# A decoder step on one core: split order, one PSUM pool, two plain gate columns, low parts on DVE, 17 groups by seven

## The chip, the cores and the metric

One core of one Trainium2 chip runs the whole program. The metric is device time in microseconds (us) of one launch; the median of three runs before the change is 1559.41 us (1559.0 to 1563.05). The core has five engines with a queue each, worked in order: TensorE (PE, matmul, with PEld for its weight loads), VectorE (DVE), ScalarE (ACT), GpSimd (POOL, which here also issues most small DMAs) and SyncE (SP, which issues the weight loads).

## The reference

A layer for 512 prompt tokens and 8 sample tokens (T = 520 columns): h = rmsnorm(x); one projection h @ w_in gives q, k, v, indexer queries, weights and key, the gate paths z_a and z_b, u, v of a gMLP, and the merge gates g_a, g_b (2048 columns each).

```python
o_a = prompt_attention(...)            # top-k by the indexer, softmax; sample_attention gathers from a paged cache
o_b = gmlp_mix(u, vb, ...)
y_a = (o_a * silu(z_a)) @ w_proj_a
y_b = (o_b * silu(z_b)) @ w_proj_b
mix = sigmoid(g_a) * y_a + sigmoid(g_b) * y_b
y   = rmsnorm(x + mix @ w_out)
```

All is float32. A product of two float32 matrices is made of three matmuls: each operand is split into a high part (float32r, rounded) and a low part (the rest), and high x high, high x low and low x high are summed in PSUM.

## The kernel before, in words

The activations stand transposed, features on partitions, as `hT_hi` and `hT_lo` (16 tiles of 128 features by 520 tokens). Weights stream in as `raw` tiles of 1 MB (1024 rows, 256 columns; three buffers, `load_raw`, on SP's queue). The work of TensorE is a flat list of chunks, built by `group` and `sgroup` and numbered in the order in which they run. A plain chunk has 8 k-tiles x 3 passes x 2 token halves = 48 matmuls of 260 columns; a plain group of 256 output columns over 2048 features has 4 chunks (192 matmuls). A group "by seven" (`by_seven`, `SEVEN`) makes the same output by Strassen's scheme (in Winograd's form): 7 chunks of 24 matmuls (168), whose weights are sums of the four quarter blocks b11, b12, b21, b22 of two raw tiles, made in place on DVE (`raw<-raw`), and whose moving operands are sums of the quarters of h. Those, forms 3, 5 and 7 (`Fh`, `Fl`) and form 6 (written over a quarter of hT), are made once by `build_forms`, some DVE sums and a split for each.

The program is one loop over chunks; iteration i issues, in this order, on every engine's queue: the split of a chunk ahead (ACT rounds `raw` to `whi`, DVE takes `wlo` = raw - whi: `hilo`; three chunks ahead in the stage by seven, `SLOOK`, two elsewhere, `LOOK`; four buffers `wspl`, so the split of chunk i+3 needs chunk i-1 done on TensorE), the evacuation of the chunk before (`pending`), chunk i's matmuls, and then one step of each running generator in `jobs` (attention, sample attention, loads, forms), in the order of their start. In the stage by seven the evacuation (`seven_after`) stands ahead of the split. So what an engine does is fixed at build time; a wait in one step holds whatever stands behind it on the same engine. Small tiles come from one pool `t` of 37 slots of 520 columns; a new tile waits until a slot is free.

PSUM: `pss` has four banks for attention and the like. The other four are `mains`: a pool of two pairs of banks (`pm`, plain chunks: both token halves, one bank each) or of four single banks (`pone`, chunks by seven). `banks` closes one pool and opens the other when the kind changes, which happens at the first chunk by seven and at the first one of the projection behind them.

Order of the chunks around the change: 92 to 107 q (8 heads); 108 to 111 z_a columns 0 and 1 (`plain_za(0)`, `evac_za`: Silu, then `gate_a` multiplies with the attention output `oT`, loaded back from DRAM by POOL, and stores to `oda`); 112 to 127 the first projection y_b = o_b @ w_proj_b (its operand `ob` is loaded and split by `loads_for_yb`, which starts with the evacuation of head 6; its results go to DRAM by `evac_yb`); 128 to 131 z_a columns 2 and 3; 132 to 257 the 18 groups by seven (z_a 4 to 7, g_b 0 to 15, g_a 0 to 15, two columns a group); 258 on the second projection y_a (operand `oa`, `loads_for_ya`), then w_out. For g_b each finished column is multiplied with y_b, loaded back from DRAM (`times_branch`). Beside chunks 108 to 123 `sample_attend` runs: for each of 8 samples POOL gathers the chosen keys and values from the cache (two indirect DMAs of about 1 us each for keys, two for values), DVE transposes the keys (`kTs`), ACT rounds them (`kTh`, line 1483), POOL subtracts (`kTl`, line 1484), TensorE multiplies (`ssP`, line 1474).

Lines that matter: 85 (all DVE work goes by `sub`, `add`, `mul`), 147 (the rounding of `hilo`), 337 (matmuls by seven), 352 (plain matmuls), 366 to 384 (`seven_after`), 1230 (`evac_yb`), 1394 (`evac_za`), 133 to 135 (`mm3`: attention).

Of the kernel before, what the change touches and what calls it, by code (L numbers as in the profile page):

```python
# [14 lines left out]
P = 128  # L15
# [25 lines left out]
WIKI_AT = 4  # L41
SEL_AT = 40
XR_AT = 10
COLS_N = NS + 2 * P
ROWS = (3, 0)
FIN = ("dve", "act", "pool", "pool")
# [13 lines left out]
def kernel(  # L60
# [31 lines left out]
    wspl = ctx.enter_context(tc.tile_pool(name="wspl", bufs=4))  # L92
    pools = {}
    dram = ctx.enter_context(tc.tile_pool(name="scratch", bufs=1, space=bass.MemoryType.DRAM))
    pss = ctx.enter_context(tc.tile_pool(name="pss", bufs=4, space=bass.MemoryType.PSUM))
    ctx.enter_context(tc.manual_schedule())
    mains = {}


    def banks(kind):  # L100
        if mains.get("kind") == kind:
            return
        if "cm" in mains:
            mains["cm"].__exit__(None, None, None)
        mains["n"] = mains.get("n", 0) + 1
        cm = tc.tile_pool(name=f"psm{mains['n']}", bufs=2 if kind == "pair" else 4, space=bass.MemoryType.PSUM)
        mains.update(kind=kind, cm=cm, pool=cm.__enter__())

    def pair_banks():
        banks("pair")  # L110
        return mains["pool"].tile([P, 2, 512], F32, name="pm")

    def one_bank():
        banks("one")
        return mains["pool"].tile([P, 512], F32, name="pone")

    xp = x_prompt[0]
    xs = x_sample.rearrange("b o d -> (b o) d")
# [132 lines left out]
    def split_steps(i, pieces):  # L251
        if i >= len(chunks) or not chunks[i]["new"]:
            return
        ch = chunks[i]
        hi = wspl.tile([P, 8, P], F32R, name="whi")
        lo = wspl.tile([P, 8, P], F32R, name="wlo")
        if ch.get("seven"):
            spl_tiles[ch["raw"], ch["step"]] = (hi, lo)
            a, b = raw_tiles[ch["raw"]], raw_tiles[ch["raw"] + 1]
            b11, b12, b21, b22 = a[:, :, :P], a[:, :, P:], b[:, :, :P], b[:, :, P:]  # L260
            step = ch["step"]
            hilo(hi, lo, (b11, b11, b12, b22, b21, b22, b21)[step])
            if step == 0:
                add(b11, b11, b12)
                add(b12, b12, b22)
            elif step == 3:
                add(b22, b11, b22)
                load_raw()
            elif step == 4:
                add(b21, b22, b21)  # L270
            elif step == 6:
                del raw_tiles[ch["raw"]], raw_tiles[ch["raw"] + 1]
                load_raw()
            return
        if ch["rows"]:
            hi, lo = (t.rearrange("p (k u) c -> p k (u c)", u=2) for t in (hi, lo))
            spl_tiles["rows", ch["kq"]] = (hi, lo)
            k0 = ch["kq"] % 2 * 4
            hilo(hi, lo, raw_tiles[ch["raw"]][:, k0:k0 + 4, :])
            if k0:  # L280
                del raw_tiles[ch["raw"]]
                load_raw()
            return
        src = raw_tiles[ch["raw"]][:, :, ch["c0"]:ch["c0"] + P]
        spl_tiles[ch["raw"], ch["u"]] = (hi, lo)
        n = 8 // pieces
        for k in range(0, 8, n):
            if ch["evac"] is packed:
                nc.scalar.activation(hi[:, k:k + n], src[:, k:k + n], AF.Copy)
                sub(hi[:, k:k + n, NIH:2 * NIH], src[:, k:k + n, :NIH], f32(hi[:, k:k + n, :NIH]))  # L290
            else:
                hilo(hi[:, k:k + n], lo[:, k:k + n], src[:, k:k + n])
            if k + n < 8:
                yield
        if ch["u"] == 1:
            del raw_tiles[ch["raw"]]
            load_raw()

    def split(i, pieces=1):
        for _ in split_steps(i, pieces):  # L300
            pass

    def rows_chunk(ch):
# [156 lines left out]
    for j in range(0, 8, 2):  # L460
        group(w_in2, C_Q + j * P, KT, rhs_h, [lz("evac_q", j), lz("evac_q", j + 1)])
    plain_za(0)
    for d in range(0, 16, 2):
        group(w_proj_b[0], d * P, 8, lambda k: ob[k], [lz("evac_yb", d), lz("evac_yb", d + 1)])
    plain_za(2)
    for j in (4, 6):
        by_seven(C_ZA + j * P, AF.Silu, [lz("gated_a", j), lz("gated_a", j + 1)])
    for x, col in (("b", C_GB), ("a", C_GA)):
        for j in range(0, 16, 2):
            by_seven(col + j * P, AF.Sigmoid, [lz("gated", x, j), lz("gated", x, j + 1)])  # L470
    for j in range(0, 16, 2):
        group(w_proj_a[0], j * P, 8, lambda k: oa[k], [lz("evac_ya", j), lz("evac_ya", j + 1)])
# [11 lines left out]
    def build_forms():  # L484
        A11, A12, A21, A22 = range(4)
        made, x6s = {}, []
        for f, r in ((1, A11), (2, A12), (4, A22), (6, A21)):
            forms[f] = lambda k, r=r: tuple(quad(t, r, k, 1)[:, 0, :] for t in (hT_hi, hT_lo))

        def T2(name, dt=F32):  # L490
            return TT(name, (P, 2, HALF), dt)

        def keep(f, k, x):
            made[f, k] = (T2("Fh", F32R), T2("Fl", F32R))
            hilo(*made[f, k], x)

        for f in (3, 5, 7):
            forms[f] = lambda k, f=f: tuple(t[:, k % 2, :] for t in made[f, k - k % 2])
        def parts(k):
            return [(f32(quad(hT_hi, r, k)), f32(quad(hT_lo, r, k))) for r in range(4)]  # L500

        for k in range(0, 8, 2):
            (h11, l11), _, (h21, l21), (h22, l22) = parts(k)
            x = T2("x5")
            sub(x, h22, h21)
            add(x, x, l22)
            sub(x, x, l21)
            keep(5, k, x)
            yield
            x = T2("x7")  # L510
            sub(x, h11, h21)
            add(x, x, l11)
            sub(x, x, l21)
            keep(7, k, x)
            yield
        while state["i"] < first7 - 4:
            yield
        for k in range(0, 8, 2):
            (h11, l11), (h12, l12), _, _ = parts(k)
            h5, l5 = (f32(t) for t in made[5, k])  # L520
            x6 = T2("x6")
            vec.scalar_tensor_tensor(x6, h5, -1.0, h11, op0=ALU.mult, op1=ALU.subtract)
            sub(x6, x6, l5)
            sub(x6, x6, l11)
            x6s.append(x6)
            x = T2("x3")
            vec.scalar_tensor_tensor(x, x6, -1.0, h12, op0=ALU.mult, op1=ALU.subtract)
            sub(x, x, l12)
            keep(3, k, x)
            yield  # L530
        while state["i"] < first7:
            yield
        for k, x6 in zip(range(0, 8, 2), x6s):
            hilo(quad(hT_hi, A21, k), quad(hT_lo, A21, k), x6)
# [703 lines left out]
    def gated(x, d):  # L1238
# [4 lines left out]
                start(times_branch(d, t))  # L1243
        return f

    def times_branch(d, t):
        yield
        mul(t, t, yl.pop(d))
        load(yl, d + 2, yd)
        nc.gpsimd.dma_start(mixd[d], t)  # L1250
# [10 lines left out]
        hilo(o[k][0], lo, f32(lo))  # L1261

    def loads_for_yb():
        for k in range(0, 8, 2):
            if k:
                yield
            load_o("b", ob, k)
            load_o("b", ob, k + 1)
            if k:
                split_o(ob, k - 2)  # L1270
                split_o(ob, k - 1)
        yield
        split_o(ob, 6)
        split_o(ob, 7)

    def loads_for_ya():
        for k in range(3):
# [44 lines left out]
    def evac_q(h):  # L1322
        def f(ps):
# [8 lines left out]
            start(attend(h, hi, lo), first=True)  # L1332
            if h == 7:
                start(sample_attend())
            if h == 6:
                start(loads_for_yb())
        return f

    def attend(h, qh, ql):
# [50 lines left out]

    def evac_za(h):
        def f(ps):
            t = TT("za", (P, T))
            nc.scalar.activation(halves(t), ps[:, :, :HALF], AF.Silu)  # L1394
            start(gate_a(h, t))
# [20 lines left out]
    def sample_attend():  # L1416
# [40 lines left out]
        for i in range(0, NS + 4, 2):  # L1457
# [20 lines left out]
            for b in (i, i + 1):  # L1478
                if b < NS:
                    t = TT("kTs", (P, 512))  # L1480
                    quads(t, fixed("k", b).rearrange("p a n -> p (a n)"))
                    yh, yl = TT("kTh", (P, 512), F32R), TT("kTl", (P, 512), F32R)
                    nc.scalar.activation(yh, t, AF.Copy)
                    nc.gpsimd.tensor_tensor(yl, t, f32(yh), op=ALU.subtract)
                    cur.append((b, (yh, yl)))
            for b in (i, i + 1):
                if b + 4 < NS:
# [184 lines left out]
        vec.scalar_tensor_tensor(x, x, sq[:, 1:2], xr["gs"], op0=ALU.mult, op1=ALU.mult)  # L1672
        nc.sync.dma_start(ys.rearrange("b (d j) -> (b d) j", j=P), x)

    evacs_of.update(evac_wi=evac_wi, evac_ki=evac_ki, evac_qi=evac_qi, evac_kv=evac_kv, evac_vb=evac_vb, evac_u=evac_u, evac_zb=evac_zb, evac_yb=evac_yb, evac_ya=evac_ya, gated_a=gated_a, gated=gated, evac_q=evac_q, evac_za=evac_za, out_cols=out_cols, out_rows=out_rows)
    load_raw()
    split(0, 2)
    h_tile(0)
# [17 lines left out]
    for i in range(len(chunks)):  # L1696
        state["i"] = i
        seven = chunks[i].get("seven")
        if not seven:
            while i > 1 and ahead < i + LOOK:  # L1700
                ahead += 1
                split(ahead)
        for f, a in pending:
            f(*a)
        while seven and ahead < i + SLOOK:
            ahead += 1
            split(ahead)
        pending = []
        ps = main_chunk(i, hook if i < 2 else None)
        ch = chunks[i]  # L1710
        if ch["last"]:
# [13 lines left out]
            start(kidx_rows_of())  # L1725
        if i == 58:
            start(gmlp_setup())
        if i == first7 - 14:
            start(build_forms())
        if i == last7 - 13:  # L1730
            start(loads_for_ya())
        if i == last7:
            for f, a in pending:
                f(*a)
            pending = []
        if i == SEL_AT:
            start(select_setup())
        for j in list(jobs):
# [11 lines left out]
    while jobs:  # L1750
        for j in list(jobs):
            if next(j, 0) == 0:
                jobs.remove(j)
    mains["cm"].__exit__(None, None, None)


_INS = ["x_prompt", "x_sample", "cache_k", "cache_v", "cache_k_idx", "page_table", "norm_in_g", "w_in",
# [24 lines left out]
```

## Time and profile before

| | |
|---|---|
| median of 3 runs | 1559.41 us |
| profiled execution, its own time | 1558.63 us |
| its span, first to last instruction | 1556.9 us |
| granted TensorE clock, mean | 0.992 |
| PE busy | 1499.0 us (96%) |
| PEld busy | 1478.4 us (95%) |
| DVE, ACT, POOL busy | 986.8 (63%), 577.2 (37%), 326.6 us (21%) |

Busy time of PE is modelled: a matmul of 260 columns has a row of 0.28 us, but the next one starts 0.12 us later, so rows overlap and a gap shorter than a row does not show as idle time. The pitch of the starts tells more.

### The profile page before, as it was taken

To read this page: it belongs to the slowest core of one execution; us is meant where nothing else is said; L and a number is where in the kernel's file an instruction comes from. 1 tells how busy PE (TensorE), PEld (TensorE's weight loads), DVE (VectorE), ACT (ScalarE), POOL (GpSimd) and SP (SyncE) were. 2 spreads that over 40 slices of the span, in tenths; PEclk is the share of its full clock that TensorE was granted. 3 is DMA by queue.
4 is the path that set the end of the run, shared out by engine and by line. 5 is a ranking of instruction groups with operands and counts; after the bars stand their busy time and mean duration, and the time that the engine had idled before them with its cause. 6 is when DMAs were issued, how large, how long until landed. Compare 5 with 4: busy or idle time off the path is not lost. (4 is left out here: it accounts for less than half of the span.)

```text
span 1556.9 us, 28370 instructions
## 1 busy us (share of the span) xinstructions
PE 1499.0 (96%) x11790; PEld 1478.4 (95%) x11790; DVE 986.8 (63%) x1854; ACT 577.2 (37%) x934; POOL 326.6 (21%) x437
## 2 busy tenths in 40 slices
PE   5999999999999999998899999999999989999997
PEld 4999999999999989998799999999999989999997
DVE  7544547988997624556467878787777765523324
ACT  6534432433222214344234444434444432322323
POOL 3000007885000220016631010110000142210112
PEclk9999999999999999999999999999999999999999
DMA  6432324546132232225645343554343495523212
GB/s 191 135 120 93 98 82 155 160 137 180 57 122 96 84 114 84 69 85 167 204 136 164 121 127 119 160 163 145 121 135 121 143 331 193 184 82 109 75 62 110
DMA packets 156580, 203.63 MB, mean 131 GB/s; under 512 B 7685, under 2 KB 138109, under 8 KB 156445
## 3 DMA queue, kind: packets, MB, share of 16 engines
q1 hardware_dynamic: 136292, 139.74, 28.6%
q0 software_dynamic: 20160, 62.09, 12.4%
q8 instruction: 92, 1.51, 0.4%
q14 instruction: 36, 0.29, 0.1%
HBM read 176.90 MB, written 24.91 MB: 130 GB/s over the span
## 5 line engine op out<-in xcount | busy, mean ns | idle before, releaser
L85 DVE TENSOR_TENSOR wlo<-raw,whi 128x1024 fp32r<-128x1024 f32 (+2 forms) x314 | 393.1, 1253 | 161.3 <-ACT whi L147 159.1
L147 ACT ACTIVATE whi<-raw 128x1024 fp32r<-128x1024 f32 (+2 forms) x314 | 319.9, 1026 | 158.2 <-PE pm L352 74.6
L352 PE MATMUL pm<-hT_hi,whi 128*128 128x260 f32 (+1 forms) x1584 | 365.5, 298 | 0.8 <-issue 0.8
L352 PE MATMUL pm<-hT_lo,whi 128*128 128x260 f32 (+1 forms) x1584 | 357.7, 293 | 4.0 <-DVE hT_lo L85 2.4
L352 PE MATMUL pm<-hT_hi,wlo 128*128 128x260 f32 (+1 forms) x1568 | 352.5, 293 | 0.8 <-issue 0.8
L352 PEld LDWEIGHTS pm<-hT_lo,whi 128*128 128x128 f32 x1584 | 254.2, 189 | 5.2 <-DVE hT_lo L85 3.2
L352 PEld LDWEIGHTS pm<-hT_hi,whi 128*128 128x128 f32 x1584 | 254.5, 190 | 1.6 <-issue 1.0
L352 PEld LDWEIGHTS pm<-hT_hi,wlo 128*128 128x128 f32 x1568 | 251.1, 189 | 1.4 <-issue 1.3
L337 PE MATMUL pone<-hT_hi,wlo 128*128 128x260 f32 x576 | 164.3, 285 | 0.1
L337 PE MATMUL pone<-hT_hi,whi 128*128 128x260 f32 x576 | 162.9, 283 | 1.1 <-ACT za L1394 1.1
L337 PE MATMUL pone<-hT_lo,whi 128*128 128x260 f32 x576 | 162.6, 282 | 0.0
L337 PE MATMUL pone<-Fh,wlo 128*128 128x260 f32 x432 | 124.7, 289 | 6.5 <-DVE wlo L85 5.6
L337 PE MATMUL pone<-Fh,whi 128*128 128x260 f32 x432 | 121.9, 282 | 0.0
L337 PE MATMUL pone<-Fl,whi 128*128 128x260 f32 x432 | 121.9, 282 | 0.0
L352 PE MATMUL pm<-oh,whi 128*128 128x260 f32 x512 | 105.6, 288 | 8.5 <-DVE c L85 5.4
L337 PEld LDWEIGHTS pone<-hT_hi,wlo 128*128 128x128 f32 x576 | 108.5, 188 | 2.1 <-DVE wlo L85 1.8
L337 PEld LDWEIGHTS pone<-hT_hi,whi 128*128 128x128 f32 x576 | 108.4, 188 | 1.3 <-ACT za L1394 1.3
L337 PEld LDWEIGHTS pone<-hT_lo,whi 128*128 128x128 f32 x576 | 108.4, 188 | 0.0
L352 PE MATMUL pm<-ol,whi 128*128 128x260 f32 x512 | 104.6, 286 | 0.0
L352 PE MATMUL pm<-oh,wlo 128*128 128x260 f32 x512 | 104.1, 285 | 0.0
L337 PEld LDWEIGHTS pone<-Fh,wlo 128*128 128x128 f32 x432 | 81.3, 188 | 11.9 <-DVE wlo L85 11.9
L85 DVE TENSOR_TENSOR raw<-raw 128x1024 f32<-128x1024 f32 x72 | 88.2, 1225 | 2.5
(498 smaller groups left out, 2718.9 us busy)
## 6 DMA issues: line engine op xcount, KB each, us to landing
raw<-in_w_in_dram SPq DMA_DIRECT2D x91, 1024.0 KB, 5.2
raw<-in_w_out_dram SPq DMA_DIRECT2D x16, 1024.0 KB, 5.4
raw<-in_w_proj_b_dram SPq DMA_DIRECT2D x8, 1024.0 KB, 6.7
raw<-in_w_proj_a_dram SPq DMA_DIRECT2D x8, 1024.0 KB, 7.0
yd<-y POOLq DMA_DIRECT2D x16, 260.0 KB
ld<-yd POOLq DMA_DIRECT2D x16, 260.0 KB
mixd<-c POOLq DMA_DIRECT2D x16, 260.0 KB
sigd<-c POOLq DMA_DIRECT2D x16, 260.0 KB
```

The source lines that it names most:

```text
L85: return f(out, *a, **k)
L147: nc.scalar.activation(hi, src, AF.Copy)
L337: nc.tensor.matmul(out, lhsT=w[:, k, :], rhs=a, start=k == 0 and j == 0, stop=k == 7 and j == 2)
L352: nc.tensor.matmul(ps[:, bank, o:o + t1 - t0], lhsT=w[:, k, :], rhs=a[:, t0:t1], start=(ch["first"] and k == 0 and j == 0), stop=(ch["last ...
```

## The change

1. In the stage by seven the split of chunk i+3 issues its rounding on ACT first, then the evacuation of chunk i-1, then the subtraction and the sums of blocks on DVE.
2. One PSUM pool of two pairs; a chunk by seven takes half a pair (one bank).
3. z_a columns 2 and 3 run ahead of the first projection; `loads_for_yb` starts with the evacuation of z_a 0 and issues its loads and splits in six steps.
4. Gate columns g_b 0 and 1 become a plain group behind the first projection; 17 groups by seven remain.
5. The keys' low parts in `sample_attend` go to DVE.
6. Forms 5 and 7 share the sum h21 + l21 (five DVE sums in place of six), and start 13 chunks ahead of the stage by seven, not 14.

The chunks become: 108 to 115 z_a 0 to 3; 116 to 131 y_b; 132 to 135 g_b 0, 1; 136 to 254 by seven; 255 on y_a.

```diff
     def pair_banks():
-        banks("pair")
-        return mains["pool"].tile([P, 2, 512], F32, name="pm")
+        return psm.tile([P, 2, 512], F32, name="pm")
     def one_bank():
-        banks("one")
-        return mains["pool"].tile([P, 512], F32, name="pone")
+        if "t" in half:
+            return half.pop("t")[:, 1, :]
+        half["t"] = pair_banks()
+        return half["t"][:, 0, :]
...
-            hilo(hi, lo, (b11, b11, b12, b22, b21, b22, b21)[step])
+            src = (b11, b11, b12, b22, b21, b22, b21)[step]
+            nc.scalar.activation(hi, src, AF.Copy)
+            yield
+            sub(lo, src, f32(hi))
...
-    def split(i, pieces=1):
-        for _ in split_steps(i, pieces):
+    def split(i, pieces=1, then=None):
+        steps = split_steps(i, pieces)
+        if then is not None:
+            next(steps, 0)
+            then()
+        for _ in steps:
             pass
...
     plain_za(0)
+    plain_za(2)
     for d in range(0, 16, 2):
         group(w_proj_b[0], d * P, 8, lambda k: ob[k], [lz("evac_yb", d), lz("evac_yb", d + 1)])
-    plain_za(2)
+    group(w_in2, C_GB, KT, rhs_h, [lz("evac_gate", 0), lz("evac_gate", 1)])
...
-            x = T2("x5")
-            sub(x, h22, h21)
-            add(x, x, l22)
-            sub(x, x, l21)
-            keep(5, k, x)
+            x, x5 = T2("x"), T2("x5")
+            add(x, h21, l21)
+            sub(x5, h22, x)
+            add(x5, x5, l22)
+            keep(5, k, x5)
             yield
-            x = T2("x7")
-            sub(x, h11, h21)
+            sub(x, h11, x)
             add(x, x, l11)
-            sub(x, x, l21)
             keep(7, k, x)
...
+    def evac_gate(d):
+        def f(ps):
+            t = TT("sg")
+            nc.scalar.activation(halves(t), ps[:, :, :HALF], AF.Sigmoid)
+            start(times_branch(d, t))
+        return f
...
     def loads_for_yb():
+        for n in range(6):
+            for k in (2 * n, 2 * n + 1):
+                if n < 4:
+                    load_o("b", ob, k)
+                if n > 1:
+                    split_o(ob, k - 4)
+            yield
...
     def evac_za(h):
         def f(ps):
+            if h == 0:
+                start(loads_for_yb())
...
-                    nc.scalar.activation(yh, t, AF.Copy)
-                    nc.gpsimd.tensor_tensor(yl, t, f32(yh), op=ALU.subtract)
+                    hilo(yh, yl, t)
...
-        for f, a in pending:
-            f(*a)
+        def follow():
+            for f, a in pending:
+                f(*a)
+            pending.clear()
         while seven and ahead < i + SLOOK:
             ahead += 1
-            split(ahead)
-        pending = []
+            split(ahead, then=follow if pending else None)
+        follow()
         ps = main_chunk(i, hook if i < 2 else None)
```

## Rows read from the trace of the kernel before

**Rows 1.** Who waited for whom, PE: us in total, times, longest.
```profile
PE pone L337 <- DVE wlo L85: 5.6, 11, 0.7
PE pm L352 <- DVE c L85: 5.4, 1, 5.4
PE oP L133 <- ACT ptAh L147: 4.3, 1, 4.3
PE ssP L1474 <- POOL kTl L1484: 3.2, 3, 1.5
...
PE pm L352 <- ACT y L1230: 3.1, 3, 1.7
...
PE ssP L1474 <- ACT kTh L1483: 2.3, 1, 2.3
...
PE pone L337 <- ACT za L1394: 1.1, 1, 1.1
```
**Rows 2.** Stretches: length, PE, PEld, DVE, ACT, POOL busy (instructions), PEclk, DMA, GB/s.
```profile
877.40:1256.50 379.10, 372.43 (x3024) 365.01 (x3024) 299.64 (x356) 168.72 (x226) 34.75 (x64) 1.00 0.45 143
990.00:1119.70 129.70, 126.17 (x1011) 122.32 (x1010) 102.43 (x121) 54.52 (x73) 12.00 (x23) 1.00 0.46 141
...
725.40:735.30 9.90, 5.62 (x29) 4.94 (x29) 6.63 (x11) 6.51 (x10) 7.74 (x7) 0.68 0.28 75
748.00:756.00 8.00, 4.03 (x27) 3.54 (x27) 5.99 (x13) 2.70 (x4) 5.83 (x6) 0.80 0.66 213
719.40:877.40 158.00, 144.01 (x1175) 141.23 (x1173) 102.55 (x184) 57.12 (x84) 60.22 (x70) 0.97 0.46 146
```
**Rows 3.** Timeline of PE, 1250 to 1269: start, us of a row, instruction.
```profile
1250.04 0.28 PE L337 MATMUL pone<-hT_hi,whi 128*128 128x260 f32 x1
...
1256.38 0.28 PE L337 MATMUL pone<-hT_hi,wlo 128*128 128x260 f32 x1
1262.03 0.77 PE L352 MATMUL pm<-oh,whi 128*128 128x260 f32 x2 [5.37 <-DVE c L85]
...
1268.46 0.40 PE L352 MATMUL pm<-oh,whi 128*128 128x260 f32 x2
```
**Rows 4.** Timeline of ACT: the first evacuation of a group by seven.
```profile
989.90 0.37 ACT L366 ACTIVATE s<-pone 128x260 f32<-128x260 f32 x1
...
1119.56 0.37 ACT L366 ACTIVATE s<-pone 128x260 f32<-128x260 f32 x1
...
1221.50 0.37 ACT L366 ACTIVATE s<-pone 128x260 f32<-128x260 f32 x1
```
**Rows 5.** Timelines of ACT and DVE inside one such group.
```profile
1006.80 0.64 ACT L380 ACTIVATE c<-c 128x520 f32<-128x520 f32 x1 [2.66 <-DVE c L85]
...
1008.42 1.23 DVE L85 TENSOR_TENSOR wlo<-raw,whi 128x1024 fp32r<-128x1024 f32 x1 [1.32 <-ACT whi L147]
```
**Rows 6.** Groups, 877 to 1260: count | busy us, mean ns | idle before.
```profile
L85 DVE TENSOR_TENSOR wlo<-raw,whi 128x1024 fp32r<-128x1024 f32 x126 | 153.7, 1221 | 76.5 <-ACT whi L147 76.5
L147 ACT ACTIVATE whi<-raw 128x1024 fp32r<-128x1024 f32 x127 | 131.8, 1052 | 72.2 <-DVE raw L85 44.7 <-PE pone L337 25.3 <-DVE zs L85 2.2
...
L85 DVE TENSOR_TENSOR raw<-raw 128x1024 f32<-128x1024 f32 x70 | 85.8, 1225 | 2.4
...
L85 DVE TENSOR_TENSOR c<-pone,s 128x260 f32<-128x260 f32 x54 | 22.8, 422 | 0.0
```
**Rows 7.** Timelines of POOL, DVE and ACT, 743 to 777.
```profile
743.78 1.71 POOL L1389 DMA_DIRECT2D oTl<-oTd  x3
...
746.80 0.69 DVE L85 TENSOR_TENSOR za<-za,oTl 128x512 f32<-128x512 f32 x1 [11.05 <-DMA oTl<-oTd]
...
776.38 0.60 ACT L1230 ACTIVATE y<-pm 128x520 f32<-128x520 f32 x1 [13.87 <-DMA oda<-za]
```
**Rows 8.** Timeline of ACT: a change of function table.
```profile
727.29 1.28 ACT L1394 ACT_TABLE_LOAD   x1
728.59 0.60 ACT L1394 ACTIVATE za<-pm 128x520 f32<-128x520 f32 x1
```

More of the change, by code (lines that the diff above doesn't have):

```diff
@@ L43 @@
 XR_AT = 10
+FORMS_AT = 13
 COLS_N = NS + 2 * P
@@ L94 @@
     dram = ctx.enter_context(tc.tile_pool(name="scratch", bufs=1, space=bass.MemoryType.DRAM))
+    psm = ctx.enter_context(tc.tile_pool(name="psm", bufs=2, space=bass.MemoryType.PSUM))
     pss = ctx.enter_context(tc.tile_pool(name="pss", bufs=4, space=bass.MemoryType.PSUM))
     ctx.enter_context(tc.manual_schedule())
[L97 to L107, printed above, removed]
+    half = {}
     def pair_banks():
-        banks("pair")
-        return mains["pool"].tile([P, 2, 512], F32, name="pm")
+        return psm.tile([P, 2, 512], F32, name="pm")
     def one_bank():
-        banks("one")
-        return mains["pool"].tile([P, 512], F32, name="pone")
+        if "t" in half:
+            return half.pop("t")[:, 1, :]
+        half["t"] = pair_banks()
+        return half["t"][:, 0, :]
     xp = x_prompt[0]
@@ L468 @@
     for x, col in (("b", C_GB), ("a", C_GA)):
-        for j in range(0, 16, 2):
+        for j in range(2 if x == "b" else 0, 16, 2):
             by_seven(col + j * P, AF.Sigmoid, [lz("gated", x, j), lz("gated", x, j + 1)])
@@ L1263, in loads_for_yb @@
     def loads_for_yb():
[L1264 to L1274, printed above, removed]
+        for n in range(6):
[5 more added lines that the diff above has]
+            yield
     def loads_for_ya():
@@ L1334, in f @@
                 start(sample_attend())
-            if h == 6:
-                start(loads_for_yb())
         return f
@@ L1673, in out_samples @@
         nc.sync.dma_start(ys.rearrange("b (d j) -> (b d) j", j=P), x)
-    evacs_of.update(evac_wi=evac_wi, evac_ki=evac_ki, evac_qi=evac_qi, evac_kv=evac_kv, evac_vb=evac_vb, evac_u=evac_u, evac_zb=evac_zb, evac_yb=evac_yb, evac_ya=evac_ya, gated_a=gated_a, gated=gated, evac_q=evac_q, evac_za=evac_za, out_cols=out_cols, out_rows=out_rows)
+    evacs_of.update(evac_wi=evac_wi, evac_ki=evac_ki, evac_qi=evac_qi, evac_kv=evac_kv, evac_vb=evac_vb, evac_u=evac_u, evac_zb=evac_zb, evac_yb=evac_yb, evac_ya=evac_ya, gated_a=gated_a, evac_gate=evac_gate, gated=gated, evac_q=evac_q, evac_za=evac_za, out_cols=out_cols, out_rows=out_rows)
     load_raw()
@@ L1727 @@
             start(gmlp_setup())
-        if i == first7 - 14:
+        if i == first7 - FORMS_AT:
             start(build_forms())
@@ L1732 @@
         if i == last7:
-            for f, a in pending:
-                f(*a)
-            pending = []
+            follow()
         if i == SEL_AT:
@@ L1753 @@
                 jobs.remove(j)
-    mains["cm"].__exit__(None, None, None)
 _INS = ["x_prompt", "x_sample", "cache_k", "cache_v", "cache_k_idx", "page_table", "norm_in_g", "w_in",
```

## The prediction, as made before the run

> **What bounds the kernel now.** TensorE's queue is the path: 96% busy, and every other engine under 64%. So I read first who PE waited for [rows 1], then the stretches that hold those waits [rows 2], then the timelines around each. The reader is to see that the waits lie in three places, 719 to 877, 877 to 1256.5 and at 1262, all of which the change touches; what PE does before chunk 108 stays as it is.
>
> The waits understate the middle place. In the stage by seven 3024 matmuls take 379.10 us [rows 2]. The undisturbed pitch is (1256.38 - 1250.04) / 53 = 0.1196 us, 53 starts lying between the two rows [rows 3], so 3024 of them need 361.7 us and 17.4 us are lost, while the waits name 5.6 (and 1.1 at its head) and busy time would show 6.7: the rows of 0.28 us overlap, and a stall of a few tenths hides under them.
>
> Why it loses: the start of a group's first evacuation recurs every (1119.56 - 989.90) / 6 = 21.61 us in the g_b groups and every (1221.50 - 1119.56) / 5 = 20.39 us in the g_a groups [rows 4], where 168 x 0.1196 = 20.09 are needed. DVE is not full: 102.43 us in 129.70 [rows 2], 17.07 per 21.61. It stands still for ACT: 76.5 us waiting for `whi`, while ACT stands 72.2 ahead of the same `whi` [rows 6]. One link shows it: ACT waits 2.66 us for DVE's sum, evacuates, only then rounds the next `whi`, and DVE waits 1.32 for that [rows 5]. The two hand the turn back and forth, because the evacuation stands ahead of the split on both.
>
> **The change, part by part.**
>
> *Rounding first.* I lay one g_b group by hand. A slot is 24 x 0.1196 = 2.87 us; at its start chunk i-1 is done, which frees both the buffer of `whi` for chunk i+3 and the evacuation. ACT: `whi` 1.05 at once. DVE: an evacuation sum 0.42 beside it, then `wlo` 1.22, ready 2.3 into the slot, and the sums of blocks at 1.23 each [rows 6]. The heaviest slot (two sums) ends 4.8 after its start, and the next `whi`, which reads the first of these sums, starts 0.7 into the next slot. The last `wlo` of any slot is done some 3.6 after the slot began, and it is wanted 8.6 after it. DVE's 17.07 per group fits in 20.09. So the 17.4 us go, all of them in the likely case. Bounds: 0, if the order does not decide, to 17.4. I take 17.4 less 1.0 for the first group, where two splits, four hT parts and a late g_b product meet: 16.4.
>
> *One group less.* A plain group has 192 matmuls for 168: 24 x 0.1196 = +2.9 us. Its Sigmoid evacuations and two products lie in the slack of ACT and DVE; if that cover were gone, no more than the two products.
>
> A change of function table stands ahead of `za`: the load takes 1.28 and `za` starts 0.02 after its end [rows 8]. Sigmoid columns ahead of Silu groups add one or two such loads to ACT, 2.6 us by the rows, in slots where ACT has over 1 us to spare: nothing on the path. The Trainium skill, "ScalarE: Activation LUTs", What ACT_TABLE_LOAD costs, asks for all uses of one table set together and prices a switch at 2.66 us, of which 1.38 is a drain. The trace shows the load and no drain. By the page ACT would lose 5.3 us, still spread over slots with 8.6 us of lead.
>
> *One PSUM pool.* At the head of the stage PE's 1.1 us for `za` [rows 1] is the closing of the old pool; it goes. At its end PE stops at 1256.38 + 0.12 = 1256.50 and starts at 1262.03 on the word of the last evacuation, 5.5 us, and the next 30 matmuls take 6.43 us to 1268.46 in place of 3.59, at the low of the two clock levels, 2.8 more [rows 3]: 8.4 us. With one pool the first chunk of y_a needs only the pair used two pairs ago. What is late next is `oa`: its last two parts are split behind the last evacuation. Without DVE's lag they are ready about 3 us after the last chunk by seven (sum 0.4, Silu or Sigmoid and two roundings on ACT 1.8, two subtractions), and k-tile 6 is wanted 6 x 6 x 0.1196 = 4.3 after it. So 8.4 goes; bounds 0 (DVE's lag stays) to 8.4.
>
> *Between 719 and 877.* PE idles 158.00 - 144.01 = 14.0 us there [rows 2], just the sum of five kinds of wait: 4.3 + 3.2 + 3.1 + 2.3 + 1.1 [rows 1].
> The 4.3 (attention head 7 waits for `ptAh`) stay. ACT is late there because DVE spread the sample queries and transposed the first two keys, both ahead of it. The split of `ob` leaves DVE at this point, about 1.3 us earlier; the first key's low part now stands on DVE between the two keys, with its wait for ACT, about 1.3 us later (half a `wlo`, and half a `whi` [rows 6]). I take 0; bounds -1.3 to +1.5. The low clock behind it, 0.68 over 9.9 us [rows 2], stays too.
> The 2.3 and 3.2 (`ssP` waits for keys' parts) start with DVE, held 11.05 us for `oTl`, which POOL issued only at 743.78 [rows 7], because its subtractions, each waiting for ACT, stood ahead of the gathers. With the subtractions gone POOL issues gathers and loads as slots come free, some ten us earlier, the two `ob` loads now ahead of `oTl` included, and DVE does not stop. Moving the subtraction adds to DVE, for each key, a wait of half a `whi` and work of half a `wlo`, 1.1 us, or 2.3 per iteration, and an iteration is 48 x 0.1196 = 5.7 or longer; PE wants the parts an iteration later, which hides it. With these waits goes the low clock at 748 to 756, (1 - 0.80) x 8.0 = 1.6 us [rows 2].
> The 3.1 (`pm` waits for `y`): one part is a `y` tile that waits 13.87 us for a slot until a store of `za`, late on POOL, has landed [rows 7]; POOL is earlier now. The other is ACT and DVE with two jobs in one iteration, forms and the sample's values. The values keep iterations 117 to 121; forms move from 118 to 123.
> `ob` itself: all eight parts are split by the end of chunk 115, one chunk before use. Their loads stand on POOL behind gathers of keys and values; if they land late, ACT and DVE stop in the split, with two chunks (11 us) of weights made ahead.
> The 1.1 for `za` is the pool's, above. So 3.2 + 3.1 + 2.3 + 1.1 + 1.6 = 11.3 goes; bounds -5 (a new stall as long as the present ones, with its slow clock) to +15.6 (the 4.3 as well).
>
> *Forms.* Four sums fewer on DVE, under plain chunks: 0; behind -1 and +1.
>
> **Sum.** -16.4 + 2.9 - 8.4 - 11.3 = -33.2 us on the profiled execution's 1558.63 (span 1556.9 and 1.7 around it): 1525.4. The median shown is 0.8 above that execution, so I say 1526.
>
> **The rivals.**
> *A, DVE is the bound by its work, not by its turn.* For: 17.07 of 20.09, and the block sums alone hold ACT 44.7 us [rows 6]. Against: PE's own need is larger, and DVE's 76.5 us of standing still exceed PE's 17.4. Then a group stays at 21.61, the trade of one group for a plain one costs 192 x 0.1196 - 21.61 = +1.4, and the end of the stage keeps half its stall: 1558.6 + 1.4 - 4.2 - 11.3 = 1544.5; 1545.
> *B, the middle stretch trades its stalls for others.* For: POOL's gathers, `ob` loads and `oT` loads now share the same iterations, and DVE takes on 16 more waits for ACT. Against: what was late was POOL, and it is relieved. Nothing gained there: 1558.6 - 16.4 + 2.9 - 8.4 = 1536.7; 1537.
> *C, slower: the halves of a pair guard each other.* If the pool's waits go by the tile and not by the bank, the second chunk of a pair cannot write its bank until the first chunk's has been read, and that reading now stands behind `whi` on ACT: 1.05 + about 0.4 for ACT's evacuations, 0.4 and DVE's lag for the others, about 1.2 each. 59 pairs x 1.2 = 71 us against the 33: about 1596. It decides from 33 / 59 = 0.56 us per pair. For: nothing in this trace writes one bank of a PSUM tile while another of it is read. Against: `hT` is written by columns while PE reads others of it, and `raw` by blocks. In this kernel's stage by seven the clock stood at 1.00 through gaps of 17.4 us in all [rows 2]; it fell only behind gaps of some 4 us and more, single or close together [rows 1, 3]. The Trainium skill, "TensorE: Matmul & The Clock Gate", A second HAM failure mode, says that cycling through PSUM banks with many micro-idles also makes the clock swing; by that rule the half-pairs would run partly at the low level and C would cost more. Here the trace speaks against it for gaps below one microsecond.
>
> **How the numbers follow.** Forecast 70%, B 13%, A 8%, C 4%, and 5% for mixtures, mostly between the forecast and B. The forecast's own spread is 1518 (the 4.3 with its slow clock goes as well: 33.2 + 4.3 + 2.8 is 40, to 1518) to 1533 (some 7 us of the three terms left over). The range runs from there to A: 1518 to 1543. A measurement here tells 0.3%, 4.7 us. Faster 0.93, same 0.02, slower 0.05.
>
> **What would show it.** In the trace after: the period of groups by seven at 20.1 in g_b and g_a alike (A: 21.6); DVE's wait for `whi` far below 76 us; no wait of `pm` for a sum `c` at the head of y_a, and no low clock there (PE's first y_a chunk at full pitch); `oTl` issued over ten us earlier relative to chunk 111, DVE's wait for it gone, `ssP` not waiting; the wait for `ptAh` still there, at about 4 us. Wrong: `pone` or `pm` matmuls waiting for evacuations in every second chunk (C), ACT waiting for `ol` landings or for slots (B), or a period that is even in both kinds of group but above 20.5.

## The result, and the profile after

| | before | after |
|---|---|---|
| median of 4 runs each | 1559.54 us (1559.0 to 1563.05) | 1620.72 us (1613.12 to 1622.27) |
| ratio | | 1.0378, 95% interval 1.0341 to 1.0415 |
| span of the profiled execution | 1556.9 us | 1620.5 us |
| granted TensorE clock, mean | 0.992 | 0.987 |

The change makes the kernel some 60 us slower (59 by the ratio, 61 by the medians); 1526 us was forecast. It is rival C, to which the prediction gave 4% and a time of 1596 us.

First the waits of PE after the change (us in total, times, longest), to be set beside [rows 1].

```profile
PE pm L338 <- DVE c L86: 30.3, 25, 2.7
PE pm L338 <- ACT s L367: 14.0, 9, 3.1
PE pm L338 <- ACT c L372: 12.2, 9, 1.4
PE pm L338 <- ACT s L369: 10.8, 8, 1.4
...
PE pm L338 <- DVE s L86: 4.4, 8, 0.7
PE oP L127 <- ACT ptAh L141: 3.5, 1, 3.5
```

The waits for `ssP`, `y` and `za` are gone, as forecast, and so is that of 5.4 us for `c` at the head of y_a; the wait for `ptAh` stays. But chunks by seven (line 338) wait in five rows 59 times, 71.7 us together: once in each pair of chunks, at its second chunk, always for an evacuation (`c`, `s`). The releasers on lines 367 to 385 are `seven_after`; line 86 is DVE's helper.

Now one such stall on the timeline, PE and ACT in order of time (start, us, instruction, idle before).

```profile
976.37 0.28 PE L338 MATMUL pm<-Fh,wlo 128*128 128x260 f32 x1
976.62 1.06 ACT L257 ACTIVATE whi<-raw 128x1024 fp32r<-128x1024 f32 x1 [1.51 <-issue]
977.59 0.37 ACT L369 ACTIVATE s<-pm 128x260 f32<-128x260 f32 x1
978.01 0.39 PE L338 MATMUL pm<-Fh,whi 128*128 128x260 f32 x1 [1.35 <-ACT s L369]
```

The first chunk of a pair ends on PE at 976.37 + 0.12. That frees a weight buffer, so ACT rounds the next `whi` (1.06 us), and only then evacuates the chunk into `s` (0.37 us). PE's second chunk, whose bank nobody reads, starts 0.05 us after that evacuation: 978.01 - 976.49 = 1.52 us lost. This is C's chain term by term.

Stretches (length, busy time of PE, PEld, DVE, ACT and POOL, PEclk, DMA share, GB/s): the middle stretch, the stage by seven, and two pieces of the stage around one stall.

```profile
720.67:887.53 166.86, 163.15 (x1367) 162.02 (x1366) 108.59 (x185) 65.17 (x94) 50.40 (x69) 0.99 0.50 164
887.53:1328.76 441.23, 369.60 (x2858) 357.58 (x2856) 294.63 (x340) 168.02 (x217) 33.57 (x62) 0.97 0.37 121
1012.00:1016.00 4.00, 1.80 (x9) 1.80 (x10) 3.24 (x4) 1.06 (x1) 0.00 (x0) 0.81 0.00 0
1016.00:1020.00 4.00, 4.00 (x28) 4.00 (x27) 1.05 (x3) 1.07 (x1) 0.00 (x0) 0.76 0.00 0
```

The stage takes 441.23 us for 2856 matmuls; at the pitch of 0.1196 [rows 3] they need 341.6, so 99.6 are lost, 1.69 per pair. Named waits are 71.7 of it. The overlap of rows (0.28 less 0.12) hides 59 x 0.16 = 9.4. The first matmul behind a stall has a row of 0.39 us in place of 0.28 (976.37 and 978.01 above), 59 x 0.11 = 6.5. The clock, 0.97 over the stage where it stood at 1.00 before [rows 2], takes by estimate 0.03 x 441 = 13. These four make 101, so with their rounding all of the 99.6 is accounted for.

The end of the stage, on PE's timeline, against [rows 3]: no stall and no slow clock in front of y_a.

```profile
1328.64 0.28 PE L338 MATMUL pm<-hT_hi,wlo 128*128 128x260 f32 x1
1328.84 0.47 PE L353 MATMUL pm<-oh,whi 128*128 128x260 f32 x2
```

**Where the time went.** All in profiled executions, in us. The anchor is the rounding of q head 6, the last one ahead of the first edit in time; on ACT's timeline, before and then after:

```profile
685.92 0.60 ACT L1327 ACTIVATE qh<-pm 128x520 fp32r<-128x520 f32 x1 [2.60 <-PE pm L352]
```
```profile
687.19 0.60 ACT L1330 ACTIVATE qh<-pm 128x520 fp32r<-128x520 f32 x1 [2.60 <-PE pm L353]
```

| piece | before | after | difference | forecast |
|---|---|---|---|---|
| start to the anchor | 685.92 | 687.19 | +1.3 | 0 |
| anchor to stage by seven, without the plain group's 192 x 0.1196 | 191.55 | 177.38 | -14.2 | -11.3 |
| the plain group in place of one by seven, 24 x 0.1196 | | | +2.9 | +2.9 |
| lost in the stage by seven | 17.4 | 99.6 | +82.2 | -16.4 |
| last chunk by seven to the end | 300.4 | 291.7 | -8.7 | -8.4 |
| sum | | | +63.5 | -33.2 |

The measured difference of the spans is 63.6. Four of the five pieces came within 3 us of the forecast; one missed by 98.6.

### The profile page after: what moved, and what is told of

The parts are those of the page before. It is cut to its first block, busy times and chain, and to the rows that moved or that the text cites. A ratio compares the mean times of both kernels' runs of the same rounds, so it can differ in the third digit from the quotient of the medians.

```text
span 1620.5 us, 28341 instructions
## 1 busy us (share of the span) xinstructions
PE 1512.1 (93%) x11814; PEld 1488.8 (92%) x11814; DVE 982.9 (61%) x1844; ACT 580.3 (36%) x929; POOL 314.3 (19%) x429
## 3 DMA queue, kind: packets, MB, share of 16 engines
q8 instruction: 92, 1.51, 0.4%
## 5 line engine op out<-in xcount | busy, mean ns | idle before, releaser
L353 PEld LDWEIGHTS pm<-hT_lo,whi 128*128 128x128 f32 x1648 | 264.2, 189 | 5.9 <-DVE hT_lo L86 3.2
L353 PEld LDWEIGHTS pm<-hT_hi,whi 128*128 128x128 f32 x1648 | 264.4, 189 | 2.6 <-issue 1.9
L353 PEld LDWEIGHTS pm<-hT_hi,wlo 128*128 128x128 f32 x1632 | 261.0, 189 | 0.9 <-issue 0.9
L141 ACT ACTIVATE whi<-raw 128x1024 fp32r<-128x1024 f32 (+2 forms) x192 | 193.4, 1009 | 94.4 <-PE pm L353 74.8
L257 ACT ACTIVATE whi<-raw 128x1024 fp32r<-128x1024 f32 x119 | 126.0, 1059 | 260.3 <-PE pm L338 128.8
L338 PE MATMUL pm<-hT_hi,whi 128*128 128x260 f32 x544 | 162.0, 298 | 34.6 <-DVE c L86 30.3
L338 PE MATMUL pm<-hT_lo,whi 128*128 128x260 f32 x544 | 158.5, 291 | 0.0
L338 PE MATMUL pm<-hT_hi,wlo 128*128 128x260 f32 x544 | 158.2, 291 | 0.0
L338 PE MATMUL pm<-Fh,whi 128*128 128x260 f32 x408 | 118.6, 291 | 37.0 <-ACT s L367 14.0
L338 PEld LDWEIGHTS pm<-hT_hi,whi 128*128 128x128 f32 x544 | 107.6, 198 | 41.2 <-DVE c L86 28.9
L338 PE MATMUL pm<-Fl,whi 128*128 128x260 f32 x408 | 115.9, 284 | 0.0
L338 PEld LDWEIGHTS pm<-hT_lo,whi 128*128 128x128 f32 x544 | 107.6, 198 | 0.0
L338 PEld LDWEIGHTS pm<-hT_hi,wlo 128*128 128x128 f32 x544 | 107.4, 198 | 0.0
```

Source lines behind the costliest of these rows:

```text
L141: nc.scalar.activation(hi, src, AF.Copy)
L257: nc.scalar.activation(hi, src, AF.Copy)
L338: nc.tensor.matmul(out, lhsT=w[:, k, :], rhs=a, start=k == 0 and j == 0, stop=k == 7 and j == 2)
L353: nc.tensor.matmul(ps[:, bank, o:o + t1 - t0], lhsT=w[:, k, :], rhs=a[:, t0:t1], start=(ch["first"] and k == 0 and j == 0), stop=(ch["last ...
```

## The experiments

Times are compared with runs of the kernel before made on the same chip at the same time, since those differ by some microseconds from one set to the next (see the end).

### The pair as one tile: three ways round it

Two pools again, all else as after the change (part 2 alone undone):

```diff
-    psm = ctx.enter_context(tc.tile_pool(name="psm", bufs=2, ...))
+    mains = {}     # banks(kind): two pairs, or four single banks, as before
     def one_bank():
-        if "t" in half:
-            return half.pop("t")[:, 1, :]
-        half["t"] = pair_banks()
-        return half["t"][:, 0, :]
+        banks("one")
+        return mains["pool"].tile([P, 512], F32, name="pone")
```

> The changed kernel with part 2 alone undone: plain chunks take pairs from a pool of two pairs, chunks by seven take single banks from a pool of four, and the pools change at both ends of the stage, as before. Theory (the halves of a pair guard each other): the stalls in every second chunk by seven go (pm<-c, pm<-s, together 71.7 us in the trace after), and with them the slow stretches of the clock; the stage by seven runs 2856 x 0.1196 = 341.6 us plus one or two, the middle keeps its 12.9 us of gain, the pools' two ends cost 1 to 6 us again: 1558.6 - 12.9 - 16.4 + 2.9 = 1532, from 1526 to 1538. Rival (the order of rounding and evacuation costs, whatever the pool): stalls of some 1.2 us at every second chunk or every chunk stay in the waits, and the time stays between 1595 and 1622.

Measured: 1526.05 us against 1560.31, ratio 0.977 (0.9738 to 0.9802). The stage by seven as a stretch, and the starts around its end on PE:

```profile
887.64:1229.53 341.89, 341.89 (x2856) 341.85 (x2856) 289.10 (x338) 166.62 (x214) 33.68 (x62) 1.00 0.49 155
```
```profile
1229.41 0.28 PE L345 MATMUL pone<-hT_hi,wlo 128*128 128x260 f32 x1
1231.22 0.48 PE L360 MATMUL pm<-oh,whi 128*128 128x260 f32 x2 [1.53 <-DVE c L86]
```

As the theory expected: 341.89 us where 341.6 are needed. PE never stops, with the same order, as many banks and the same instructions; the rival, that the order costs, falls. What the two pools still cost is 1.5 us here and 1.7 us ahead of the stage, where its first chunk waits for the plain gate's evacuation. The reading of one bank beside the writing of another costs nothing here. What costs is that two banks are one tile, so that the program's own wait between a reading and the next writing (the guard) holds for both. The Trainium skill, "PSUM — Partial Sum Buffer", PSUM bank collisions raise a hardware error, asks for guards by bank (or by quadrant of a bank). This run agrees as far as time goes: with a guard for each bank the stage takes 341.89 us, with one for two banks 441.23.

Part 2 alone, on the kernel before (one pool, halves; 18 groups; evacuation ahead of the split):

```diff
-        banks("one")
-        return mains["pool"].tile([P, 512], F32, name="pone")
+        if "t" in half:
+            return half.pop("t")[:, 1, :]
+        half["t"] = pair_banks()
+        return half["t"][:, 0, :]
```

> The kernel before with part 2 alone: one pool of two pairs, a chunk by seven takes half a pair; 18 groups, evacuation ahead of the split as before. Theory (halves guard each other): every second chunk waits for the evacuation of the one before it, 63 pairs; here the evacuation stands first on ACT and DVE, so the wait is that of one evacuation and its issue, 0.5 us and more where the engine is still at an earlier split (up to 1.2): 63 x 0.5 to 1.2 = +32 to +76, less the 5 to 8 us at the stage's two ends: 1583 to 1627. Rival (the one pool alone costs nothing, it is the order that does): 1558.6 - 8.4 = 1550, 1548 to 1559, with no wait in every second chunk.

Measured: 1630.96 us, ratio 1.0445 (1.0425 to 1.0464), above the expected upper end by 4 us; the rival, that one pool alone costs nothing, falls. Three of PE's starts in its stage by seven:

```profile
968.02 0.39 PE L330 MATMUL pm<-Fh,whi 128*128 128x260 f32 x1 [0.48 <-ACT s L361]
974.63 0.39 PE L330 MATMUL pm<-hT_hi,whi 128*128 128x260 f32 x1 [0.61 <-DVE c L85]
...
1003.09 0.39 PE L330 MATMUL pm<-hT_hi,whi 128*128 128x260 f32 x1 [2.30 <-DVE c L85]
```

With the evacuation first, the guard's price falls where ACT evacuates and is free: 0.48 us idle, where the changed order has 1.35. Where DVE evacuates, little is won: 0.61 here, 0.52 to 0.61 in the changed order, and 2.30 in both where DVE is still at an earlier split. The stage takes 458.77 us in place of 379.03, 1.27 more per pair; with the changed order it is 441.23 in place of 341.89, 1.68 per pair. (Against the need of the matmuls alone it is (458.77 - 361.7) / 63 = 1.54 and 1.69.) So part 2 is dear by itself, and part 1 makes it somewhat dearer, by the rounding that it puts ahead of ACT's evacuations.

A whole pair for each chunk by seven, of which it uses one bank, and the four banks handed out crosswise, both on the changed kernel:

```diff
-        if "t" in half:
-            return half.pop("t")[:, 1, :]
-        half["t"] = pair_banks()
-        return half["t"][:, 0, :]
+        return pair_banks()[:, 0, :]          # whole pair
...
+        q = half.setdefault("q", [])          # crosswise
+        if not q:
+            a, b = pair_banks(), pair_banks()
+            q += [a[:, 0, :], b[:, 0, :], a[:, 1, :], b[:, 1, :]]
+        return q.pop(0)
```

> The changed kernel, but a chunk by seven takes a whole pair and writes only its first bank: two chunks in flight and not four, and no tile that is written and read in different banks at once. Theory (the guard goes by the tile): chunk i waits only for the evacuation of chunk i-2, a whole slot of 2.87 us old, so nearly all of the 71.7 us go; ACT's and DVE's delays up to 2.3 us into the slot stay hidden: 1525 to 1540. Rival (what costs is that a pair comes free only as a whole, so that four banks act as two): here banks are two deep as well, and the stalls stay: 1600 and more.

> The changed kernel, the four banks handed out crosswise: first bank of pair A, first of B, second of A, second of B. Four banks are in flight, but a chunk shares its pair with the chunk two before it, not with the one just before. Theory (a write into a pair waits for the last reading of the same pair): the reading it waits for is that of chunk i-2, which is a slot of 2.87 us old and done 1 to 2 us before: stalls of at most a few us in all, 1517 to 1528, as the whole pairs gave (1520). Rival (writing one bank while the other of the pair is in any way in use costs): stalls as in the changed kernel, every second chunk and more: above 1590.

Measured: whole pairs 1520.08 us against 1560.31, 0.9731 (0.9703 to 0.9758); crosswise 1516.8 against 1551.29, 0.9776 (0.9762 to 0.9789). The stages by seven of the two:

```profile
885.63:1229.23 343.60, 342.78 (x2858) 342.11 (x2856) 290.60 (x340) 168.03 (x217) 33.57 (x62) 1.00 0.49 154
```
```profile
880.13:1223.69 343.56, 342.74 (x2858) 342.05 (x2856) 290.58 (x340) 168.03 (x217) 33.55 (x62) 1.00 0.48 154
```

Two us lost in each, not 99.6; both rivals fall, and whole pairs come in 5 us below the expected range. Half the depth is enough: a slot has 2.87 us, and in both kernels the reading of a chunk is done 0.6 to 2.4 us after its last matmul, but for a few chunks of the first and the last two groups (2.8 to 3.5). And a second bank may be written when the other bank of its pair was read a slot earlier. What costs is to write one half of a tile while the other half, filled in the slot just before, still waits to be read. That settles the cause.

### The order by itself

Part 1 alone on the kernel before:

```diff
-            hilo(hi, lo, (b11, b11, b12, b22, b21, b22, b21)[step])
+            nc.scalar.activation(hi, src, AF.Copy)
+            yield                                   # then the evacuation
+            sub(lo, src, f32(hi))
```

> The kernel before with part 1 alone: in the stage by seven ACT rounds first, then the evacuation, then DVE's low part; two pools, 18 groups. The prediction's step: 17.4 us lost in the stage go but for about one, and the lag of DVE at its end with them (0 to 6 us of the 8.4): 1558.6 - 16.4 - 0 to 6 = 1536 to 1542, the period of a g_b group 20.1 us. Rival A (DVE's work is the bound): the period stays at 21.6 and the time at 1555 to 1560. Rival (the order itself costs, since the evacuation now comes 1 us later): slower than 1560.

Measured: 1540.10 us, 0.9865 (0.9849 to 0.9882). Its stage by seven, and the head of y_a:

```profile
880.86:1245.12 364.26, 364.26 (x3024) 364.21 (x3024) 306.50 (x359) 174.70 (x225) 34.76 (x64) 1.00 0.48 153
```
```profile
1246.79 0.48 PE L359 MATMUL pm<-oh,whi 128*128 128x260 f32 x2 [1.51 <-DVE c L85]
```

The stage has 364.26 us for 361.7 needed: 2.6 lost where 17.4 were. Rival A falls. And the head of y_a, still with two pools, waits 1.51 us instead of 5.37 with no slow clock behind it; the time behind the last chunk by seven is 293.2 us against 300.4. So 7.2 of the 8.7 us won behind the stage, which the prediction booked (as 8.4) to the one pool, come with the order alone: DVE's lag, not the change of pools, made most of that stall.

### The middle stretch: parts 3, 4 and 5

Parts 3 and 4 alone on the kernel before (columns, `loads_for_yb`, the plain gate group, as in the diff of the change), and part 5 alone (the keys' low parts by `hilo`):

> The kernel before with parts 3 and 4 alone: z_a 2 and 3 ahead of the first projection, loads_for_yb at z_a 0 in six steps, g_b 0 and 1 as a plain group, 17 groups by seven; keys' low parts still on POOL, two pools, old order. The prediction's step: one group less +2.9, the columns' order nothing of its own (the waits of ssP for keys and of pm for y stay, since POOL is as late as before): 1560.3 + 2.9 = 1563, from 1559 to 1567. Rival (the order of the columns, not POOL's relief, gave the 12.9 us of the middle): 1560.3 + 2.9 - 12.9 = 1550.

> The kernel before with part 5 alone: the keys' low parts of the sample attention on DVE in place of POOL. The prediction's step: POOL is relieved, so oTl is issued some ten us earlier, DVE's wait of 11 us for it goes, the ssP waits of 3.2 and 2.3 go, the low clock behind them (1.6), and most of the wait of pm for y (3.1): 1560.3 - 7 to 10 = 1550 to 1553. Rival (POOL's place does not set these waits, or DVE takes on as many): 1558 to 1563 with the waits of ssP still there.

Measured, against 1551.29: parts 3 and 4 1550.67, 0.9997 (0.9988 to 1.0006), not told from no change; part 5 1546.57, 0.9969 (0.9957 to 0.9981), a gain of 4.7 where 7 to 10 were expected. The expected times started from 1560.3, and the kernel before takes 9 us less in this set, so only the differences can be compared: for parts 3 and 4 +2.7 was expected (-1.3 to +6.7) and -10 by the rival, and -0.6 came; that 1550.67 lies by the rival's 1550 is chance. PE's waits in the first:

```profile
PE ssP L1478 <- ACT kTh L1487: 6.1, 1, 6.1
PE ssP L1478 <- POOL kTl L1488: 3.8, 3, 1.7
PE spT L1513 <- DVE sprob L85: 2.7, 1, 2.7
PE oP L133 <- ACT ptAh L147: 1.8, 1, 1.8
```

and in the second, with its DVE and POOL between 700 and 800:

```profile
PE oP L133 <- ACT ptAh L147: 5.8, 1, 5.8
PE pm L352 <- ACT y L1230: 3.3, 2, 1.7
PE ssP L1474 <- ACT kTh L147: 1.3, 1, 1.3
...
DVE za L85 <- DMA oTl<-oTd: 5.4, 1, 5.4
POOL kg L1425 <- PE ssP L1474: 11.0, 1, 11.0
```

From the anchor to the stage by seven (the plain group taken off) the first takes 191.6 us and the second 189.3, against 191.55: gains of 0 and 2.2, where both together give 11.8 with two pools (the first kernel above) and 14.2 after the change. The sum was right, its parts were not. Moving the columns removes the waits for `y` and shortens that of `ptAh` by 2.5, but DVE's stall for `oTl` is longer than before (14.7 us, 11.05 [rows 7]) and `ssP` waits 9.9 us instead of 5.5. Relieving POOL alone leaves POOL itself standing 11.0 us ahead of a gather of keys, until `ssP` has run, so `oTl` is issued only 1.7 us earlier relative to the anchor: 56.2 us behind it in place of 57.9 [rows 7], and 43.8 with both (743.78, 735.60 and 730.94, on POOL's timelines, less the anchors 685.92, 679.38 and 687.19). The key's low part on DVE makes the `ptAh` wait 1.5 us longer (4.3 to 5.8), the very bound that the prediction gave; the columns moved, with the split of `ob` gone from there, make it 2.5 shorter, where 1.3 was given.

Parts 3 and 4 undone in the good kernel (whole pairs, so 18 groups by seven again):

> The kernel that gives each chunk by seven a whole pair (1520), with parts 3 and 4 undone: z_a 2 and 3 behind the first projection, loads_for_yb at head 6, all 18 groups by seven. The prediction's step (a plain group costs 24 x 0.1196 = 2.9 us more, the columns' order nothing): 1517, from 1514 to 1521. Rival (the order of the columns carries a part of the gain of the middle): waits of pm for y or of the first chunk by seven come back, 3 to 9 us with their low clock: 1521 to 1527.

Measured: 1521.70 us, 0.9809 (0.9796 to 0.9822), to be set beside the crosswise kernel of the same set, 0.9776 and 1516.80 us: 4.9 us slower, in spite of a group more by seven, and above the expected range (they also differ in how the banks are handed out, which makes no difference in the stage: 343.60 and 343.56). From the anchor to the stage it takes 185.0 us, a gain of 6.5, where the crosswise kernel gains 13.6. The columns' order carries some 7 us of the middle; the "nothing of its own" of the expectations fails here. The rival was right in size, but less so in its waits: `pm` waits 0.9 us for `y`; the rest is `oP`, 5.8 us for `ptAh` instead of 3.5, and `ssP`, 2.2 us where it did not wait.

### The stall that the prediction left

The prediction read `oP`'s wait for `ptAh` as ACT's delay behind the sample queries' casts and the first two keys on DVE. On the crosswise kernel, the keys one iteration later, or casts and keys both:

```diff
                     vec.tensor_copy(qd[j][...], ql[hl][...])
+        yield                              # keys later
...
             nc.gpsimd.memset(f32(t), 0.0)
         yield
+        yield                              # both later
```

> The kernel with the banks handed out crosswise once more, so that the two kernels beside it can be compared on one chip: 0.976 to 0.980 of the kernel before, as first measured (0.9776).

> The crosswise kernel, and the sample attention's first two keys one iteration later than the spread of its queries. The prediction's reading of the stall of oP (3.5 us for ptAh): ACT stands 7.3 us for the first transposed key, which DVE makes behind 3.4 us of casts, and whi, za and ptAh stand behind it on ACT; with the keys an iteration later ACT goes straight to whi, the 3.5 us go, and the slow clock behind them (0.92 over 40.6 us, 3.2 us) with them: 5 to 7 us faster than the crosswise kernel. Rival (the keys only meet the next tight step, or za and its table load alone make ptAh late): within 2 us of the crosswise kernel, with a stall of oP or ssP of 2 us and more left.

> The crosswise kernel, and the spread of the sample queries and all behind it one iteration later, so that casts and first keys stay in one step. Prediction's reading: the step no longer meets attention head 7's copies, 3.5 us and the slow clock go: 4 to 7 us faster than the crosswise kernel. Rival (the step of casts and two keys holds ACT for 7 us wherever it stands): a stall of whi or of another evacuation of 2 to 5 us in the iteration behind: within 2 us of the crosswise kernel.

Measured, against 1556.89: crosswise again 1522.16, 0.9777 (0.9755 to 0.98); keys later 1515.37, 0.9736 (0.9713 to 0.9759); both later 1517.24, 0.9743 (0.9718 to 0.9767). The same stretch in the crosswise kernel and with the keys later:

```profile
719.40:760.00 40.60, 37.10 (x311) 36.26 (x310) 31.72 (x61) 18.99 (x28) 27.38 (x35) 0.92 0.65 214
```
```profile
719.40:760.00 40.60, 40.60 (x370) 40.37 (x369) 31.01 (x57) 18.23 (x28) 24.68 (x30) 1.00 0.74 245
```

Without the 3.5 us PE is never idle in it and the clock stays at 1.00. From the anchor to the stage by seven the time falls from 201.4 to 194.2 us. By the medians the two variants are 6.8 and 4.9 us faster than the crosswise kernel, as expected. The intervals of the ratios overlap a little, but no run with the keys later (1510.3 to 1516.9) is as long as any of the crosswise kernel beside it (1518.2 to 1523.8); the stall is gone in both variants, and the reading holds. Keys later is the version to keep (its profiled span, 1508.6 us, is the shortest seen, 7.2 below that of the first crosswise run, 1515.8; neither has the spell near 552 of the last section): 2.6% under the kernel before, and by estimate 0.9736 / 1.0378 = 0.938 of the changed one. The whole pairs' 0.9731 comes from another set and is not told from it.

## Why the prediction was wrong

The failed step is *One PSUM pool*: "With one pool the first chunk of y_a needs only the pair used two pairs ago." It asked what the pool does where kinds of chunks meet, and put at nothing what half a pair does inside the stage. The runs show in its place that the second chunk of every pair waits for the evacuation of the first: 59 waits, 71.7 us by name and 99.6 us lost, where the same instructions with four single banks lose 0.3 us. The mechanism stood there as rival C, with nearly the right price (1.2 us per pair; the named waits are 71.7 / 59 = 1.22, the time lost is 1.69) and a right point of decision (0.56 us). Wrong was its chance. It rested on `hT` and `raw`, which are written in one part while another is read. Those are tiles in SBUF; that nothing in the trace did the same in PSUM was noted, and then weighed too lightly. Why the one is free and the other is not was not tried; the runs show it for PSUM alone. The other half of the error is what the step was thought to win: 8.4 us, where the order alone gives 7.2. Beside that, 71 us at stake call for a look at the guard, or for four single banks.

C's own time, 1596, was 25 us short: the overlap of rows (9.4), the longer first rows (6.5) and the clock (13, an estimate) were not in it. On the clock the prediction held that it fell only behind gaps "of some 4 us and more", and that the trace speaks against a fall "for gaps below one microsecond". The timeline of PE after the change repeats seven stalls in every two groups, 0.61, 1.35, 0.52, 0.52, 1.36, 1.36 and 2.3 us. Three of them:

```profile
1005.85 0.39 PE L338 MATMUL pm<-Fh,whi 128*128 128x260 f32 x1 [1.36 <-ACT c L372]
1014.20 0.39 PE L338 MATMUL pm<-hT_hi,whi 128*128 128x260 f32 x1 [2.33 <-DVE c L86]
...
1022.38 0.36 PE L338 MATMUL pm<-hT_hi,whi 128*128 128x260 f32 x1 [0.61 <-DVE c L86]
```

Behind the one at 1014.20 the clock is 0.76 in the stretch 1016 to 1020 shown above: for part of it at the low of its two levels. It fell so behind eight of the ten stalls of 2.2 to 3.1 us in the stage, and behind none of the 49 shorter ones. So single stalls well under the 4 us of the prediction went ahead of a fall here, and C's stalls were not all as short as one microsecond. Nor does the trace of the kernel before speak so clearly against short gaps as the prediction says. Near 552, ahead of all edits, PE stands six times within 6 us for 0.2 to 1.15 us each, 3.1 us in all, and the clock is low behind it:

```profile
552.00:558.00 6.00, 2.88 (x15) 1.96 (x14) 1.88 (x2) 1.55 (x2) 4.00 (x5) 1.00 0.02 0
558.00:562.00 4.00, 3.96 (x21) 3.95 (x21) 0.05 (x1) 1.06 (x1) 0.00 (x0) 0.57 0.86 259
```

The Trainium skill, "TensorE: Matmul & The Clock Gate", A second HAM failure mode, has a clock that swings under frequent micro-idles while PSUM banks are cycled. The trace after the change agrees that it swings, though behind the long stalls only; the prediction named this rule and set it aside.

Step by step:

- *Rounding first*, -16.4: right. -14.8 by itself (2.6 lost where 17.4 were), and -17.1 with four free banks (341.89 for 341.6).
- *One group less*, +2.9: right on this order. On the old order the trade costs 192 x 0.1196 - 21.61 = 1.4, as rival A had it, and the kernel with parts 3 and 4 alone shows +1.3 (its stage and the plain group against the stage before).
- *A change of table* ahead of the gate columns: hidden, as said: two loads of 1.28 us (906.18 and 946.39 on ACT) lie in the stage with four free banks, and PE does not stop there.
- *One PSUM pool*, -8.4 at the end of the stage: -8.7, most of it by the order; and inside the stage, where nothing was booked, some 99 us lost.
- *Middle*, -11.3: -14.2 after the change, -13.6 with whole pairs and crosswise, -13.1 crosswise again, -11.8 with two pools. Right in sum, wrong in its working: neither part gives it alone.
- *Forms*, 0: not tried by itself; no wait for them is seen.
- With the guard out of the way the crosswise kernel takes 0.9777 of the kernel before, which of the 1559.41 us of the kernel before is 1524.6; the forecast was 1526. That it fits is partly luck: the sum of the middle came about in another way than was worked out.

## What to carry to other kernels

Where a change lets two users share a tile, ask of every place, not only of the seam that it is to mend, who now waits for whom; here a wait by the tile cost one evacuation, and whatever stood ahead of it on its engine, at every second use. Book a stall to the cause that ends last only after asking which other edit removes it: the pools got credit for what the order did. And parts that relieve one another's queues have no price of their own; price them together.

## What was not expected of the hardware

Executions of one kernel lie some 6 us apart (keys later: 1510.3 and 1511.1; 1515.4 to 1516.9). Some profiled ones hold a spell near 552 in which PE waits a few times for nothing that the profile shows, with a lower clock behind it, and some don't; this is why each ratio above is taken against runs of its own set. Stretch 540 to 560, kernel before, then keys later:

```profile
540.00:560.00 20.00, 16.84 (x125) 15.91 (x124) 4.26 (x4) 2.61 (x3) 13.26 (x15) 0.96 0.30 86
```
```profile
540.00:560.00 20.00, 20.00 (x169) 20.00 (x168) 4.42 (x5) 3.68 (x4) 13.42 (x14) 1.00 0.42 134
```

16.84 us busy of 20 at clock 0.96, and 20.00 at 1.00, in a stretch that no edit touches. Its cause stays open.
